# Attention on one core: product 2 of weights and V by seven smaller products, and VectorE's sums placed anew over a batch's four periods

## The chip, the core and the metric

The kernel runs on one core of a Trainium2 chip. PE is TensorE (matmuls), PEld its weight loads, DVE is VectorE, ACT is ScalarE, POOL is GpSimd, SP is SyncE, which here only issues DMAs. The metric is device time in microseconds (us), from the kernel's start to its end. One execution was profiled; the profile's "span" runs from its first to its last instruction.

## What is computed

Attention without a mask, for 8 batches of 2048 positions of width 512, in float32 at the borders:

```python
scores = q @ k.transpose(0, 2, 1) / sqrt(512)
weights = softmax(scores, axis=-1)
return weights @ v
```

## The kernel before

All products run on 16-bit copies of the inputs. Exponentials are taken without a maximum being subtracted, and rows are divided by their sum at the end; a column of ones beside V makes those sums.

**Two levels of seven products.** A product of two matrices, each cut into 2 x 2 blocks, is made by seven block products instead of eight, at the price of sums of blocks beforehand and of results afterwards (Strassen's method in Winograd's form). `Group` does it for scores, `Pair` for weights and V. A `Group` covers 2 x 128 keys and 1024 queries; each of its seven products is two matmuls of 512 columns (line 309). A `Pair` covers two query tiles of 128 and all of V; each of its seven products is eight matmuls of 256 columns (line 406; 257 where the column of ones goes along). The sums come before: `k_sums` (lines 185 to 188, in K's own tiles, one call for each of four quarters of K), `q_sums` (202 to 205), `v_sums` (219 to 222), `p_sums` of the exponentials (360 to 363). All of them run on DVE. A second level, `Fine` and `fine`, makes product 1 of the two pairs `a` and `b` of a period together: the two pairs' tiles and the two halves of V's block form a 2 x 2 scheme of their own, seven products of four matmuls with 128 columns (line 508), in four stages s1 to s4. Its sums are `a_sums` (486 to 489, into the tiles si) and `vi_sums` (233 to 236, into the tiles ti). Between the stages ACT copies parts of a PSUM bank (lines 516, 519, 523), and DVE adds two of them back (525, 528).

**Periods.** The main loop (line 776) runs over g = 0 to 31; four of them are a batch (`NQT` = 4). Period g makes the weights-and-V products of its two pairs, and beside them four `Group`s for the queries that come next. A period has 28 slots (`NS`). In each slot the loop issues, in this order: a product of the current or the previous group by `QORDER`; the exponential of the right half at the third position; the sums of `sums_of(g, slot)`; one product of a pair by `ORDER` (`pv`); and `prefetch`, which issues the next batch's loads and transposes by `PLAN` and, through a queue `background`, the sums of K:

```python
QORDER = ((0, 1), (1, 7), (0, 5), (0, 6), (1, 4), (0, 3), (0, 2))
ORDER = {
    1: "a7'", 3: "b7'", 5: "a4'", 7: "b4'", 8: "s1", 10: "a5", 11: "s2", 13: "b5", 14: "s3",
    16: "a3", 17: "s4", 18: "b3", 20: "a6", 22: "a2", 24: "b6", 26: "b2",
}
```

A pair (0, n) in `QORDER` is product n of the group begun in these seven slots, (1, n) one of the group before; "a7'" is product 7 of pair a of the period before. g = 0, 30 and 31 have orders of their own without `fine`. The schedule is manual: each engine executes its instructions in the order in which the program issues them. So an instruction that waits holds up everything behind it on its engine.

**What follows on the products.** Product 7 of a group is followed by a DVE add (331), product 3 by another (334); the two fill the tile cz, whose exponential (line 245, 1024 columns) ACT takes two positions later. Line 334 also empties the bank qz, of which there is one: product 5 of the next group starts in it. Line 331 reads the bank in which product 4 goes on. After products of a pair come reciprocals of the row sums (435, 441, 469), scaled copies on ACT (415) and the "final" on DVE (418: scale and add to the output tile o). When both halves of a tile are there, SP stores it (425).

**Loads.** POOL issues all loads of Q, K and V for the next batch (124, 211); Q and K go through two `stage` buffers, and SP issues the DMA that transposes a stage buffer into qraw or kraw (150). A stage buffer is free for the next load when its transpose has landed. `PLAN` puts these steps at (period of the batch, slot): K's quarters 0 to 3 are transposed at (1, 0), (1, 8), (1, 20) and (2, 7); K's third quarter is loaded at (1, 8), V's second at (1, 12). `KSUMS` adds four sums of K's quarters 0 to 3 to the queue at (1, 10), (1, 20), (2, 6) and (2, 20), and slots 2, 8, 10, 14, 16, 24 and 26 take one sum each from it.

**Start.** Batch 0 has its own beginning (lines 651 to 774): warm-up matmuls (697) on a zeroed tile, transposes on PE (137, 160), plain score tiles (252, 268), and a queue of sums that `step` takes from, among them the first of `v_sums`. In g = 0 the sums follow the table `SUMS0`.

Of the kernel before, what the change touches and what calls it, by code (L numbers as in the profile page):

```python
# [12 lines left out]
def kernel(  # L13
# [21 lines left out]
    nc = tc.nc  # L35
    P = 128
# [16 lines left out]
    CH = 4  # L53
    NCH = NKB // CH
    H = D // 2
    VP = D + 8
    TP = H + 8
    NG = NJ // 2
    NE = 6
    NI = NJ // 2  # L60
# [7 lines left out]
    opool = ctx.enter_context(tc.tile_pool(name="opool", bufs=6))  # L68
    small = ctx.enter_context(tc.tile_pool(name="small", bufs=2))
    czpool = ctx.enter_context(tc.tile_pool(name="czpool", bufs=2))  # L70
    psum = {}
    for name, bufs in (("qx", 2), ("qy", 1), ("qz", 1), ("px", 2), ("pz", 2)):
        psum[name] = ctx.enter_context(
# [7 lines left out]

    ctx.enter_context(tc.manual_schedule())

    ident32 = const.tile([P, P], F32)
    ident_dram = nc.inline_tensor(np.eye(P, dtype=np.float32), name="attn_identity")
    nc.scalar.dma_start(out=ident32[:], in_=ident_dram.ap())
    ident = const.tile([P, P], F16)

# [10 lines left out]
    vt2 = const.tile([P, NJ, H], F16, name="vt2")  # L101
    vt4 = const.tile([P, NJ, H], F16, name="vt4")
    si = {n: const.tile([P, NI, P], F16, name=f"si{n}") for n in (1, 2, 4)}
    ti = {n: const.tile([P, NI, P], F16, name=f"ti{n}") for n in (1, 2, 3, 4)}
    ci = const.tile([P, 2, P], F32, name="ci")
    staged = {}
    pts = {}

# [103 lines left out]

    def v_sums(b, c):
        vh = vraw[b % 2]
        js = slice(c * CH // 2, (c + 1) * CH // 2)
        b11, b12 = vh[:, js, 0, 0:H], vh[:, js, 0, H:D]
        b21, b22 = vh[:, js, 1, 0:H], vh[:, js, 1, H:D]
        return [
            lambda: sub(vt1[:, js, 0:H], b12, b11),
            lambda: sub(vt2[:, js], b22, vt1[:, js, 0:H]),  # L220
            lambda: sub(b12, b22, b12),  # L221
            lambda: sub(vt4[:, js], b21, vt2[:, js]),  # L222
        ]

    def vi_blocks(b):
        vh = vraw[b % 2]
        lo, hi = slice(0, NI), slice(NI, NJ)
        return vh[:, lo, 0, 0:P], vh[:, lo, 0, P:H], vh[:, hi, 0, 0:P], vh[:, hi, 0, P:H]

    def vi_sums(b):  # L230
        b11, b12, b21, b22 = vi_blocks(b)
        return [
            lambda: sub(ti[1][:], b12, b11),
            lambda: sub(ti[2][:], b22, ti[1][:]),
            lambda: sub(ti[3][:], b22, b12),
            lambda: sub(ti[4][:], b21, ti[2][:]),
        ]

    def new_p(sp):
# [234 lines left out]
            self.final(self.o1[:, H:D], self.x[:, 0:H], self.r1)  # L474
            self.store_first()

    def a_blocks(g):
        left = pts[g // 2][0][0]
        ca, cb = columns(g, "a"), columns(g, "b")
        lo, hi = slice(0, NI), slice(NI, NJ)  # L480
        return left[:, lo, ca], left[:, hi, ca], left[:, lo, cb], left[:, hi, cb]

    def a_sums(g):
        a11, a12, a21, a22 = a_blocks(g)
        return [
            lambda: add(si[1][:], a21, a22),
            lambda: sub(si[2][:], si[1][:], a11),
            lambda: sub(a21, a11, a21),
            lambda: sub(si[4][:], a12, si[2][:]),
        ]  # L490

    def fine(g, stage):

        a11, a12, a21, a22 = a_blocks(g)
        b11, b12, b21, b22 = vi_blocks(g // NQT)
        if stage == 1:
            for w in "ab":
                pairs[g, w] = Fine(g, w)
                pairs[g, w].x = bank("px")
        xa, xb = pairs[g, "a"].x, pairs[g, "b"].x  # L500

        def product(n, dst):
            lhs, rhs = {
                1: (a11, b11), 2: (a12, b21), 3: (si[4], b22), 4: (a22, ti[4]),
                5: (si[1], ti[1]), 6: (si[2], ti[2]), 7: (a21, ti[3]),
            }[n]
            for j in range(NI):
                nc.tensor.matmul(  # L508
                    dst, lhs[:, j, :], rhs[:, j, :],
                    start=(n == 1 and j == 0), stop=(j == NI - 1), skip_group_check=True,  # L510
                )

        if stage == 1:
            product(1, xb[:, 0:P])
            product(5, xb[:, P:H])
            nc.scalar.copy(out=xa[:, 0:H], in_=xb[:, 0:H])
        elif stage == 2:
            product(6, xb[:, 0:P])
            nc.scalar.copy(out=ci[:, 0, :], in_=xb[:, 0:P])
            product(2, xa[:, 0:P])  # L520
        elif stage == 3:
            product(7, xb[:, 0:P])
            nc.scalar.copy(out=ci[:, 1, :], in_=xb[:, 0:P])
            product(3, xa[:, P:H])
            nc.vector.tensor_add(xa[:, P:H], xa[:, P:H], ci[:, 0, :])
        else:
            product(4, xb[:, 0:P])
            nc.vector.tensor_add(xb[:, P:H], xb[:, P:H], ci[:, 1, :])

    pairs = {}  # L530

    def pv(g, which):
        if which[0] == "s":
            return fine(g, int(which[1]))
        g -= which.endswith("'")
        if which[1] == "1" and which[-1] != ">":
            pairs[g, which[0]] = Pair(g, which[0])
        part = {"<": (0, NJ // 2), ">": (NJ // 2, NJ)}.get(which[-1], ())
        pairs[g, which[0]].product(int(which[1]), *part)
# [2 lines left out]

    ORDER = {
        1: "a7'", 3: "b7'", 5: "a4'", 7: "b4'", 8: "s1", 10: "a5", 11: "s2", 13: "b5", 14: "s3",
        16: "a3", 17: "s4", 18: "b3", 20: "a6", 22: "a2", 24: "b6", 26: "b2",
    }
    FIRST = "a1< b1< a1> a5 b1> a3 a2 a6 - b5 - b3 b2 b6".split()
    ALONE = "a7' b7' a4' b4' a1 a5 b1 a3 b5 a6 b3 a2 a7 b6 a4 b2".split()
# [25 lines left out]
    ):  # L574
        PLAN.setdefault((qt_, slot_), []).append(what_)

    KSUMS = {(1, 10): 0, (1, 20): 1, (2, 6): 2, (2, 20): 3}
    background = deque()

    def prefetch(g, slot):  # L580
        b, qt = divmod(g, NQT)
        if (g, slot) == (0, 12):
            nc.gpsimd.memset(vraw[1][:, :, 1, D:D + 1], 1.0)
        for kind, what, c in PLAN.get((qt, slot), ()):
            if b + 1 < B:
                if kind == "load":
                    load_v(b + 1, c) if what == "v" else load(what, b + 1, c)
                else:
                    dma_transpose(what, b + 1, c)
        if (qt, slot) in KSUMS and b + 1 < B:  # L590
            background.extend(k_sums(KSUMS[qt, slot]))
        if background and slot in ((2, 8, 10, 14, 16, 24, 26)):
            background.popleft()()

    def sums_of(g, slot):

        if g == 0:
            return [first_sum(x) for x in SUMS0.get(slot, "").split()]
        todo = []
        inner = g < NP - 2  # L600
        bs = (8, 9, 10, 13) if inner else (7, 9, 11, 13)
        if inner and slot in (6, 7, 11, 12):
            todo.append(a_sums(g)[(6, 7, 11, 12).index(slot)])
        if slot in bs:
            todo.append(p_sums(g, "b")[bs.index(slot)])
        early = (20, 23, 25, 27) if g == NP - 2 else (19, 23, 25, 27)
        if slot in early and g + 1 < NP:
            todo.append(p_sums(g + 1, "a", 0, NJ if g % 2 == 0 else NE)[early.index(slot)])
        if slot in (4, 5) and g % 2 == 0:
            late = p_sums(g, "a", NE)  # L610
            todo.extend(late[0:2] if slot == 4 else late[2:4])
        sp = g // 2 + 2
        if slot in (23, 25, 27) and g % 2 == 1 and sp < NP // 2:
            todo.append(q_sums(sp)[(slot - 23) // 2])
        if slot == 6 and g % 2 == 0 and g < NP - 2:
            todo.append(q_sums(sp - 1)[3])
        if g % NQT == 0 and slot in VSUMS:
            n, c = divmod(VSUMS.index(slot), NCH)
            todo.append(v_sums(g // NQT, c)[n + 1])
        if g % NQT == NQT - 1 and g + 1 < NP:  # L620
            if slot in (14, 15, 16, 17):
                todo.append(v_sums(g // NQT + 1, slot - 14)[0])
            if slot in (18, 20, 21, 22):
                todo.append(vi_sums(g // NQT + 1)[(18, 20, 21, 22).index(slot)])
        return todo

    SUMS0 = {
        2: "v02", 3: "v03", 4: "q3", 5: "a0", 6: "a1", 8: "a3", 9: "a2",   # L630
        11: "v12 v13", 12: "v20 v21", 13: "v22", 14: "b0 v23", 15: "v30", 16: "b1 v31", 17: "v32",
        18: "v33", 19: "b3", 20: "k02", 21: "b2", 22: "A0", 23: "k12 A1", 24: "A2", 25: "k22 A3",
        26: "k32", 27: "t0 t1 t2 t3",
    }

    def first_sum(x):
# [3 lines left out]
        if x[0] == "q":  # L640
            return q_sums(1)[n]
        if x[0] == "t":
            return vi_sums(0)[n]
        return {
            "a": lambda: p_sums(0, "a", NG), "b": lambda: p_sums(0, "b"), "A": lambda: p_sums(1, "a")
        }[x[0]]()[n]

    TILES = (0, 2, 4, 5, 7, 9, 11, 13)
    VSUMS = (0, 1, 2, 3, 14, 15, 16, 17, 18, 20, 21, 22)

    warm = ti[4][:].rearrange("p j d -> p (j d)")
    nc.vector.memset(warm, 0.0)
    nc.gpsimd.memset(vt1[:, :, H:H + 1], 1.0)
    nc.gpsimd.memset(vraw[0][:, :, 1, D:D + 1], 1.0)

# [93 lines left out]
    for slot in range(14):  # L749
# [3 lines left out]
            background.extend(p_sums(0, "a", 0, NG))  # L753
            background.append(v_sums(0, 0)[0])
        if slot == 7:
            background.extend((v_sums(0, 1)[0], v_sums(0, 0)[1], v_sums(0, 1)[1]))
        if at == 0:
            cur = Group(0, 6 + n)
        if old == 0:
# [70 lines left out]
```

## Time and profile before

| | us |
|---|---|
| median of three runs | 799.06 |
| lowest and highest | 798.89, 799.32 |
| the profiled execution | 800.54 |
| its span | 798.7 |
| period g = 2 to 28, each | 24.16 |
| busy: PE, PEld | 791.7, 538.6 |
| busy: DVE, ACT, POOL | 622.2, 587.2, 72.2 |

In the profile an instruction's line is its place in the kernel's file; a row of the timeline gives start, duration, engine, line, operation, tiles (written <- read), shape and how many were merged, and in brackets the idle time of the engine before it and what ended it. The TensorE clock was granted in full (1.000). Matmuls are pipelined: a row's duration is longer than the time from its start to the next start, and it is the latter that counts. Period g starts at 63.34 us for g = 1 and at 88.43 for g = 2, and so on every 24.16.

### The profile page before, as it was taken

How to read it: one execution, taken by the hardware profiler on the slowest of the kernel's cores; microseconds unless marked ns; L12 is line 12 of the kernel's file. 1: busy time of each engine (PE TensorE's matmuls, PEld its weight loads, DVE VectorE, ACT ScalarE, POOL GpSimd, SP SyncE). 2: the span in 40 equal slices, each digit the busy share in tenths (PEclk: the TensorE clock that was granted, in tenths of full speed). 3: DMA queues.
4: the chain of work that ended last, by engine and by line, in shares of the span. 5: the costliest groups of instructions: out<-in, count | busy, mean ns of one | idle time of the engine just before them, and what ended most of it. 6: DMA issues, size and time to landing. Idle time of an engine off the chain costs nothing.

```text
span 798.7 us, 15575 instructions
## 1 busy us (share of the span) xinstructions
PE 791.7 (99%) x5878; PEld 538.6 (67%) x5878; DVE 622.2 (78%) x1426; ACT 587.2 (74%) x1107; POOL 72.2 (9%) x106
## 2 busy tenths in 40 slices
PE   9999999999999999999999999999999999999998
PEld 6556666666666666666666666666666666666676
DVE  2787869869698687977879787797878878788673
ACT  4677777877777787777777777777778777778842
POOL 4011010101100110001100111001110101000000
PEclk9999999999999999999999999999999999999999
DMA  9989993989929999389975799578994789910112
GB/s 221 177 144 160 196 181 86 168 141 193 189 57 179 163 195 172 74 165 155 202 146 105 150 178 193 116 126 148 188 205 87 144 150 195 160 53 32 49 60 101
DMA packets 188155, 115.90 MB, mean 145 GB/s; under 512 B 122288, under 2 KB 170800, under 8 KB 188080
## 3 DMA queue, kind: packets, MB, share of 16 engines
q0 software_dynamic: 49648, 49.29, 42.5%
q1 hardware_dynamic: 138144, 65.29, 36.8%
q8 instruction: 46, 0.75, 0.4%
q10 hardware_dynamic: 288, 0.33, 0.1%
q14 instruction: 29, 0.24, 0.1%
HBM read 100.73 MB, written 33.55 MB: 168 GB/s over the span
## 4 chain that ended last, share of the span: by engine, by line
PE 97%; DVE 1%; ACT 1%; issue 0%; DVEq 0%; ACTq 0%
PE t L309 45%; PE t L406 42%; PE t L508 6%; PE t L252 2%; PE tr L160 1%; PE tr L137 1%; PE t L697 0%; PE t L268 0%; DVE o L418 0%; DVE cz L334 0%; ACT left L245 0%; DVE vt L222 0%; DVE vh L221 0%; DVE s L360 0%; ACT o L415 0%
## 5 line engine op out<-in xcount | busy, mean ns | idle before, releaser
L309 PE MATMUL t<-qraw,kraw 128*128 128x512 f16 x728 | 197.0, 379 | 0.1
L406 PEld LDWEIGHTS <-s 128*128 128x128 f16 x1536 | 150.2, 98 | 57.6 <-issue 0.5
L245 ACT ACTIVATE left<-t 128x512 f16<-128x512 f32 (+1 forms) x260 | 156.1, 603 | 34.2 <-PE t L309 28.7
L415 ACT ACTIVATE o<-t,r 128x256 f32<-128x256 f32 x256 | 115.7, 481 | 62.6 <-DVE r L435 28.5
L406 PE MATMUL t<-vt,s 128*128 128x257 f16 (+1 forms) x1024 | 133.0, 273 | 0.0
L245 ACT ACTIVATE right<-cz 128x1024 f16<-128x1024 f32 x122 | 129.3, 1060 | 2.1 <-DVE cz L331 1.8
L309 PE MATMUL t<-qs,ks 128*128 128x512 f16 x488 | 130.6, 379 | 0.0
L309 PEld LDWEIGHTS <-kraw 128*128 128x128 f16 x976 | 93.0, 98 | 50.7 <-issue 0.7
L406 PEld LDWEIGHTS <-right 128*128 128x128 f16 x1024 | 100.2, 98 | 37.2 <-issue 0.5
L418 DVE SCALAR_TENSOR_TENSOR o<-t,r,o 128x256 f32<-128x256 f32 x192 | 92.2, 481 | 39.8 <-PE t L406 23.5
L325 ACT COPY cz<-t 128x512 f32<-128x512 f32 x120 | 70.2, 585 | 64.3 <-PE t L309 61.2
L331 DVE TENSOR_TENSOR cz<-t,cz 128x512 f32<-128x512 f32 x122 | 83.9, 688 | 36.7 <-PE t L309 36.3
L334 DVE TENSOR_TENSOR cz<-t,cz 128x512 f32<-128x512 f32 x122 | 84.0, 689 | 22.6 <-PE t L309 21.7
L309 PEld LDWEIGHTS <-ks 128*128 128x128 f16 x732 | 69.1, 98 | 46.7 <-issue 0.2
L320 ACT COPY t<-t 128x512 f32<-128x512 f32 x120 | 69.0, 575 | 20.0 <-PE t L309 17.7
L406 PE MATMUL t<-vh,left 128*128 128x256 f16 x560 | 72.9, 273 | 0.0
L309 PE MATMUL t<-qraw,ks 128*128 128x512 f16 x244 | 72.6, 379 | 0.0
L309 PE MATMUL t<-qs,kraw 128*128 128x512 f16 x244 | 72.6, 379 | 0.0
L328 ACT COPY cz<-t 128x512 f32<-128x512 f32 x122 | 70.8, 580 | 0.0
L406 PEld LDWEIGHTS <-left 128*128 128x128 f16 x560 | 54.8, 98 | 20.0
L406 PE MATMUL t<-vh,s 128*128 128x257 f16 x512 | 66.7, 273 | 0.4 <-ACT o L415 0.4
L406 PE MATMUL t<-vt,right 128*128 128x256 f16 x512 | 66.2, 273 | 0.3 <-DVE o L418 0.3
(85 smaller groups left out, 821.6 us busy)
## 6 DMA issues: line engine op xcount, KB each, us to landing
out_dram<-o SPq DMA_DIRECT2D x127, 256.0 KB, 3.0
vh<-in_v_dram POOLq DMA_DIRECT2D x32, 512.0 KB, 9.9
stage<-in_q_dram POOLq DMA_DIRECT2D x28, 512.0 KB, 6.9
stage<-in_k_dram POOLq DMA_DIRECT2D x28, 512.0 KB, 6.8
right<-in_q_dram POOLq DMA_DIRECT2D x2, 512.0 KB, 10.0
right<-in_k_dram POOLq DMA_DIRECT2D x2, 512.0 KB, 12.3
first<-in_q_dram SPq DMA_DIRECT2D x2, 256.0 KB, 3.5
cz<-in_q_dram SPq DMA_DIRECT2D x2, 256.0 KB, 4.8
```

Source lines behind the costliest of these rows:

```text
L245: nc.scalar.activation(out=out_, in_=in_, func=EXP, scale=inv_sqrt_d)
L252: nc.tensor.matmul(st[:], kops[c][0][:, n, dc, :], qraw[0][:, half * NT:(half + 1) * NT, dc, :], start=(dc == 0), stop=(dc == ND - 1),)
L309: nc.tensor.matmul(dst[:], lhs[:, j, dc, :], rhs[:, :, dc, :], start=(n in (1, 5) and dc == 0), stop=(dc == 1), skip_group_check=True,)
L320: f(out=self.y[:], in_=self.x[:])
L325: f(out=self.cz[:, 1, :], in_=self.z[:])
L328: nc.scalar.copy(out=self.cz[:, 0, :], in_=self.x[:])
L331: nc.vector.tensor_add(self.cz[:, 1, :], self.x[:], self.cz[:, 1, :])
L334: nc.vector.tensor_add(self.cz[:, 0, :], self.z[:], self.cz[:, 0, :])
L406: nc.tensor.matmul(dst[:, 0:width], lhs(j), rhs(j), start=(first and j == 0), stop=(j == NJ - 1), skip_group_check=True,)
L415: nc.scalar.activation(out=out_, in_=src, func=COPY, scale=r[:])
L418: nc.vector.scalar_tensor_tensor(out=out_, in0=src, scalar=r[:], in1=out_, op0=MULT, op1=ADD)
L508: nc.tensor.matmul(dst, lhs[:, j, :], rhs[:, j, :], start=(n == 1 and j == 0), stop=(j == NI - 1), skip_group_check=True,)
```

## The change

Product 2 of both pairs is made like product 1: `fine` gets an index s of the V half (0 for product 1, 1 for product 2), and the stages t1 to t4 (s = 1) take the place of a2 and b2. They stand at slots 21, 23, 25 and 27, and their results lie in the banks that a2 and b2 used. The final of line 418 that followed a2 and b2 follows stages t3 and t4. `a_sums` runs a second time a period, on the other half of the exponentials (in place there, too), into the same tiles si. `vi_sums` also runs for the second half; the tiles ti double in size, except that the third is now written into V's own tile, over a block that nothing reads any more (for the last batch, into the other buffer of V). The small float32 tile ci goes; its part is played by the left half of pair a's output tile. To make room in memory, the rows of V's tile get 514 elements instead of 520 (1028 bytes instead of 1040), those of vt1 258 instead of 264, and the two identity tiles and the warm-up tile share their memory with ti.

The sums of DVE are placed anew. `v_sums` works on halves (512 x 2 elements) instead of quarters, so there are half as many instructions, each twice as long. The sums of K leave the queue `background` and get fixed slots: quarter 0 at slots 11, 14, 15, 16 of period 1; quarter 1 at slots 18 and 20 of period 1 and 0 and 3 of period 2; quarter 2 at 11, 15, 18, 20 of period 2; quarter 3 at 0, 2, 4, 6 of period 3. `q_sums` move by one to three slots, the early `p_sums` of odd periods to slots 18, 21, 22 and 23. At the start, the second first-sum of V (half 1) is in the queue where the sum of quarter 1 was. The diff, cut to its core:

```diff
-    VP = D + 8
-    TP = H + 8
+    VP = D + 2
+    TP = H + 2
...
-    ti = {n: const.tile([P, NI, P], F16, name=f"ti{n}") for n in (1, 2, 3, 4)}
-    ci = const.tile([P, 2, P], F32, name="ci")
+    ti = {}
...
     def v_sums(b, c):
-        js = slice(c * CH // 2, (c + 1) * CH // 2)
+        js = slice(c * NI, (c + 1) * NI)
...
+    def t3_inner(b):
+        return vi_blocks(b + 1 if b + 1 == B else b)[1]
+
+    def vi_sums(b, s):
         b11, b12, b21, b22 = vi_blocks(b)
...
+                ti[n] = ipool.tile([P, 2, NI, P], F16, tag=f"t{n}", name=f"ti{n}")[:]
+        ti[3] = t3_inner(b)
+        at = lambda x: x[:, s]
         return [
+            lambda: sub(at(ti[1]), at(b12), at(b11)),
+            lambda: sub(at(ti[2]), at(b22), at(ti[1])),
+            lambda: sub(at(ti[3]), at(b22), at(b12)),
+            lambda: sub(at(ti[4]), at(b21), at(ti[2])),
         ]
...
-    def a_blocks(g):
-        left = pts[g // 2][0][0]
+    def a_blocks(g, s):
+        left = pts[g // 2][0][s]
...
-    def fine(g, stage):
+    def fine(g, s, stage):
...
+        pa, pb = (pairs.setdefault((g, w), Fine(g, w)) for w in "ab")
         if stage == 1:
+            for p in (pa, pb):
+                if s == 0:
+                    p.x = bank("px")
+                else:
+                    p.y = bank("pz")
+        xa, xb = (pa.y, pb.y) if s else (pa.x, pb.x)
...
-            nc.scalar.copy(out=ci[:, 0, :], in_=xb[:, 0:P])
+            nc.scalar.copy(out=pa.o2[:, 0:P], in_=xb[:, 0:P])
...
-            nc.vector.tensor_add(xa[:, P:H], xa[:, P:H], ci[:, 0, :])
+            nc.vector.tensor_add(xa[:, P:H], xa[:, P:H], pa.o2[:, 0:P])
+            if s:
+                pa.after2()
...
+            if s:
+                pb.after2()
...
-        16: "a3", 17: "s4", 18: "b3", 20: "a6", 22: "a2", 24: "b6", 26: "b2",
+        16: "a3", 17: "s4", 18: "b3", 20: "a6", 21: "t1", 23: "t2", 24: "b6", 25: "t3", 27: "t4",
...
-    KSUMS = {(1, 10): 0, (1, 20): 1, (2, 6): 2, (2, 20): 3}
+    KSUMS = {
+        divmod(slot, NS): (c, n)
+        for c, slots in (
+            (0, (39, 42, 43, 44)), (1, (46, 48, 56, 59)), (2, (67, 71, 74, 76)), (3, (84, 86, 88, 90))
+        )
+        for n, slot in enumerate(slots)
+    }
...
         if (qt, slot) in KSUMS and b + 1 < B:
-            background.extend(k_sums(KSUMS[qt, slot]))
-        if background and slot in ((2, 8, 10, 14, 16, 24, 26)):
-            background.popleft()()
+            c, n = KSUMS[qt, slot]
+            k_sums(c)[n]()
...
+        if g % 2 == 0 and sp < NP // 2:
+            put((2,), q_sums(sp)[2:])
+        if g % 2 == 1 and sp + 1 < NP // 2:
+            put((24, 26), q_sums(sp + 1))
+        if g % 2 == 0:
+            put((4, 4, 5, 5), p_sums(g, "a", NE))
+        if inner:
+            put((6, 7, 11, 12), a_sums(g, 0))
+            put((14, 17, 21, 22), a_sums(g, 1))
+        if g % 2 == 0 and sp < NP // 2:
+            put((7,), q_sums(sp)[3:])
+        put((8, 9, 10, 13) if inner else (7, 9, 11, 13), p_sums(g, "b"))
+        if g + 1 < NP:
+            if g % 2 == 0:
+                put((20 if g == NP - 2 else 19, 23, 25, 27), p_sums(g + 1, "a"))
+            else:
+                put((18, 21, 22, 23), p_sums(g + 1, "a", 0, NE))
+        if qt == 0:
+            put((0, 3), (v_sums(b, 0)[1], v_sums(b, 1)[1]))
+            put((15, 16), (v_sums(b, 0)[2], v_sums(b, 1)[2]))
+            put((18,), v_sums(b, 0)[3:])
+            if inner:
+                put((7, 11, 21, 17), vi_sums(b, 1))
+        if g == 1:
+            put((0, 2, 4, 6), vi_sums(0, 1))
+        elif qt == 1:
+            put((0,), v_sums(b, 1)[3:])
+        if qt == NQT - 1 and g + 1 < NP:
+            put((16, 18), (v_sums(b + 1, 0)[0], v_sums(b + 1, 1)[0]))
+            put((11, 14, 21, 23), vi_sums(b + 1, 0))
...
         if slot == 7:
-            background.extend((v_sums(0, 1)[0], v_sums(0, 0)[1], v_sums(0, 1)[1]))
+            background.extend((v_sums(0, 1)[0], v_sums(0, 0)[1]))
```

## The prediction

> **What bounds the kernel now.** I read the page first, then busy time by period, the PE timeline of one period, what PE waits for, and last the queues of DVE and DMA around the sums that move. A period is one value of g (28 slots); four make a batch, called periods 0 to 3 here, and "+17.0" means 17.0 us after a period's first matmul.
>
> ```profile
> PE 791.7 (99%) x5878; PEld 538.6 (67%) x5878; DVE 622.2 (78%) x1426; ACT 587.2 (74%) x1107; POOL 72.2 (9%) x106
> ```
>
> PE is the bound, and by its spacing it is at its floor. In the PE timeline a product of eight 256-column matmuls (line 406, 421.84 to 422.72) takes 0.87 us, so 109 ns each, and four of 128 columns (line 508, 409.84 to 410.07) take 0.224 us, so 56 ns each:
>
> ```profile
> 409.84 0.39 PE L508 MATMUL t<-vh,left 128*128 128x128 f16 x4
> 410.07 0.39 PE L508 MATMUL t<-ti,si 128*128 128x128 f16 x4
> 410.29 1.03 PE L309 MATMUL t<-qs,ks 128*128 128x512 f16 x4
> ...
> 421.84 1.04 PE L406 MATMUL t<-vh,left 128*128 128x256 f16 x8
> 422.72 1.03 PE L309 MATMUL t<-qs,ks 128*128 128x512 f16 x4
> ```
>
> From period g=2 to g=28 every period is 24.16 us long, to 0.01, with no PE wait that the profile names. The waits it names lie at the start, for instance:
>
> ```profile
> PE t L508 <- DVE si L489: 0.5, 1, 0.5
> PE t L406 <- ACT o L415: 0.4, 1, 0.4
> ```
>
> So removed PE time is gained in full, and new time appears only where a result comes after its slot. DVE is the engine to look at: busy time by period, for periods 0 and 1 of one batch (columns: us, PE, PEld, DVE, ACT, POOL busy, clock, DMA share, GB/s):
>
> ```profile
> 136.74:160.90 24.16, 24.16 (x182) 16.44 (x180) 21.35 (x52) 18.44 (x35) 2.22 (x3) 1.00 0.83 154
> 160.90:185.06 24.16, 24.16 (x182) 16.43 (x181) 16.97 (x38) 18.44 (x35) 2.22 (x3) 1.00 0.97 154
> ```
>
> **Second product by seven.** In 29 periods (g=1 to 29) two products 2 go, 16 matmuls x 109.2 ns = 1.747 us, and 28 matmuls x 55.9 ns = 1.564 us come. Gain 0.183 x 29 = **5.3 us**. That holds if the weight loads (98 ns a row, line 508) stay hidden, as under the first product's 28. The Trainium skill ("TensorE: Matmul & The Clock Gate", Back-to-back issue gap) speaks against it: streams of a weight load and a 128-column matmul are said to sustain about 81 ns a matmul. By that, an estimate, the t stages would cost 2.27 us, a loss of 15. The trace disagrees: 56 ns between the same kind of operands, so I keep 5.3.
>
> **What DVE and ACT get.** Per period DVE gets four 512-element f16 sums (0.335 us apart, e.g. 411.25 to 411.59) and two adds of 0.21: 1.76 us; period 0 also four sums for V's lower half (1.34) and one q sum (0.60), and twelve V sums of 0.335 become five of 0.60 (-1.0). So period 0 goes from 21.35 to about 24.0 of 23.97 us by busy rows, which count some 0.09 us after each instruction in which the next could already run (0.69 long, 0.60 from start to start); by starts (0.60, 0.39, 0.335, 0.21, 0.08) it is 22.1. It fits, barely. Walking the queue by these starts, the last add and final of stage t4 end 1.6 to 1.8 us into the next period. The first result needed there, line 331 of slot 1, ends at about +3.1; PE needs it at +3.47 (product 4, slot 4). ACT gets 0.36+0.28+0.27 us a period; each copy of a t stage ends 0.25 to 0.4 us before the matmul that overwrites its source. I charge none of this, with 0 to 5 us as bound (7 crossings into period 0, 29 t stages; nothing below zero, since nothing is freed). The row pitch of V falls from 1040 to 1028 bytes, which no row shows; nearest is the 257-column row at the 256-column price. I take 0, at most 1 us on a V load.
>
> **K's sums move past a DMA.** This decides. Sums that a background queue fed at fixed slots get fixed places. For K's second quarter of the next batch the first sum (line 185) goes from slot 26 of period 1 to slot 18. What it reads is written by the transpose that SP issues at slot 8. Of batch 1, SP's timeline, and the DMA issues of a window around 169.2 (last number: us from issue to landing):
>
> ```profile
> 161.62 1.83 SPq L150 DMA_TRANSPOSE kraw<-stage  x1
> 166.81 2.07 SPq L425 DMA_DIRECT2D out_dram<-o  x2
> 169.01 13.10 SPq L150 DMA_TRANSPOSE kraw<-stage  x2
> ```
>
> ```profile
> kraw<-stage SPq DMA_TRANSPOSE x1, 13.4
> ```
>
> It lands at 182.4, **+21.5**. The DVE timeline shows when slot 18 comes (the reciprocal of line 469 closes it) and when the old order read it:
>
> ```profile
> 177.88 0.17 DVE L469 RECIPROCAL r<-t 128x1 f32<-128x1 f32 x1 [0.94 <-PE t L406]
> 178.38 0.69 DVE L334 TENSOR_TENSOR cz<-t,cz 128x512 f32<-128x512 f32 x1 [0.33 <-PE t L309]
> ...
> 185.94 0.42 DVE L185 TENSOR_TENSOR ks<-kraw 128x512 f16<-128x512 f16 x1
> ```
>
> Now it was read at +25.0; after the change DVE reaches it at +17.1 and stands still. The same windows give issue plus landing for batches 0 to 6, as offsets in period 1: 14.9, 21.5, 20.4, 21.4, 19.7, 20.1, 20.9. Batch 0 is early (5.2 us of transfer); the six others wait 2.6 to 4.4 us. Behind the sum stands line 334 of slot 19, which empties the bank qz that product 5 of slot 23 starts in. Product 5 was at 181.15 (+20.25); without a2 (0.87) and with t1 (0.45) it is at +19.83. With the transpose landing at L the bank is free at L + 0.02 + 0.35 + 0.69 + 0.06 = L + 1.12 (75.33 to 75.35 in batch 0; a sum and its neighbour's start; line 334; DVE's end to PE's start at 77.05 to 77.11). So PE loses L - 18.71. Then DVE still has a6's final, the second K sum, one si sum and one early sum (0.39 + 0.335 + 0.335 + 0.46) ahead of line 331, which ends at L + 3.2; ACT's exp of cz (1.06) waits for it, and t2's copy stands behind that until L + 4.5, while t3's product 7, which overwrites the copy's source, is due at L + 3.7: another 0.8. At the landings of before: (2.8 + 1.7 + 2.7 + 1.0 + 1.4 + 2.2) + 6 x 0.8 = 11.7 + 4.8 = **16.5 us**.
>
> L itself moves. The transpose of K's first quarter (161.62) is behind the store of o1 on SP; that store follows the last final, 1.3 us later than now. The loads of K's third and V's second quarter wait for its landing and take the DMA engines while our transpose runs. They end up to 1.3 us later; L moves by 0 to 1.3. I take 0.7, since part of the shift lets our transfer go first: 6 x 0.7 = 4.2. Sum **20.7 us**, bounds 16.5 to 24.3.
>
> **Start.** V's first sums now take halves. The second, at 38.08, needs all four V loads; the last is issued at 15.27 and lands 24.8 us later, at 40.0:
>
> ```profile
> vh<-in_v_dram POOLq DMA_DIRECT2D x1, 512.0 KB, 24.8
> ```
>
> DVE stands from 38.3 to 40.1 in front of the copy at 38.56, whose bank a plain tile of 40.52 needs: 0.9 us of PE, then line 331 at 45.0 instead of 43.05 and ACT's exp behind it: I count **1.2** (0.5 to 2). Later in g=0 V's sums are 0.3 us shorter, taken off the 0.9 us of PE gaps at 56 to 60; in g=1 K's first sum moves behind the si sum that PE waited for at 76: another -0.35 of 0.9.
>
> **Sum:** -5.3 + 20.7 + 1.2 - 0.3 - 0.35 = **+15.9 us**. The profiled execution took 800.54 us (span 798.7 and 1.8 around it), 1.5 over the median of the three runs; I add the difference to the median: 799.06 + 15.9 = **815.0**.
>
> **Rivals.**
> 1. *The transpose lands in time* (13%): the other side. In batch 0 the two loads didn't fall on it and it landed at +14.9. If the loads start after it, because their release comes some 2.5 us later, the stall is nil below L = 18.7 and its echo soon after: 799.06 - 5.3 + 0.55 = 794.3. For it: the release does move later; against: by 1.3 us, and SP's place for our transpose, +8.1, stays.
> 2. *It lands part of the way earlier* (10%): each us is 6 us; 797 to 807.
> 3. *DVE and ACT are too full as well* (11%): 7 crossings into period 0 with 0.3 us of margin and 29 t stages: up to 5 more with the landings at their late end, 820 to 828.
> 4. *Weight loads show in the t stages* (1%): 28 x 98 ns against 1.747 us is +1.0 a period, +29 instead of -5.3: 849. Line 508's 56 ns excludes it unless operands differ.
> 5. *The clock drops in the long stall* (4%): at the very start the 512-column matmuls of line 697 come 0.43 us apart against 0.216 later, so a cold spell of some 3.4 us costs 1.7; twice (batches 1 and 3, 3.5 us alone): 818. The Trainium skill (same page, What's actually happening) has the clock halve after an idle window of about 3.4 us; no stall in this trace is that long.
>
> **Numbers.** Forecast (61%): 807 to 820. Range 801 to 824: it leaves out rival 1, the upper part of 3, rival 4 and some of 2. Faster by over 0.2% (the bound of what a measurement here tells from no change): rival 1 and a little of 2, 0.14; within: 0.03; slower: 0.83.
>
> **What would show it.** In the profile after: line 185 on DVE with idle before it, released by DMA kraw<-stage, six times 2.5 to 5 us; PE waiting on DVE line 334 (or ACT) six times, once a batch in period 1; other periods 23.97 us long; line 219 waiting for vh's DMA at 38. If the long periods are not period 1, or line 185 doesn't wait, the forecast is wrong; if all periods are over 23.97, rival 3 holds.

## The result and the profile after

The changed kernel takes 825.33 us (median of four runs, 824.14 to 829.15) beside 798.97 for the kernel before: a ratio of 1.0337, 95% interval 1.0302 to 1.0372. It is slower by 26.4 us. The direction was forecast, with 815.0; the time lies just outside the range given, 801 to 824. The profiled execution took 824.57 us, with a span of 822.5 against 798.7, so the trace has 23.8 us to explain.

The page of the changed kernel shows PE no longer full, and a DMA in the chain that ended last:

```profile
PE 792.6 (96%) x6226; PEld 537.8 (65%) x6226; DVE 677.8 (82%) x1568; ACT 609.1 (74%) x1194; POOL 72.1 (9%) x106
PE 79%; DMA 16%; DVE 3%; ACT 1%; issue 1%; POOL 0%; DVEq 0%; ACTq 0%
```

Lines from the changed kernel carry its own numbers: 317 was 309 (score products), 342 and 339 were 334 and 331 (the adds into cz), 414 was 406, 519 was 508, 477 was 469 (reciprocal), 497 was 489 (a sum of `a_sums`), 530 was 519 (copy in stage 2), 253 was 245 (exponential); 185 is still K's first sum.

Period 3 of batch 0 and periods 0 and 1 of batch 1 of the changed kernel (g = 3 to 5; the columns are us, then PE, PEld, DVE, ACT and POOL busy, the clock, the DMA share and GB/s):

```profile
116.49:140.50 24.01, 24.01 (x195) 16.41 (x193) 21.22 (x51) 19.24 (x39) 0.74 (x1) 1.00 0.54 108
140.50:164.61 24.11, 24.11 (x195) 16.41 (x193) 23.07 (x54) 19.18 (x39) 2.22 (x3) 1.00 0.81 154
164.61:191.68 27.07, 24.34 (x196) 16.40 (x193) 20.08 (x48) 19.24 (x39) 3.70 (x5) 1.00 0.93 158
```

Only period 1 is long, once a batch: 28.11, 27.07, 28.55, 30.03, 27.15, 26.90 and 27.78 us in batches 0 to 6; all others of g = 1 to 29 are 24.01 or, in period 0, 24.11. What PE waited for, in the order engine, tile and line, total us, times, longest:

```profile
PE t L317 <- DVE cz L342: 19.2, 7, 4.2
PE t L519 <- ACT o L530: 3.0, 5, 0.6
```

Seven waits for the add that frees bank qz, and five for the copy of stage t2. The transpose of K's second quarter in batch 1 (DMA issues at its start), the DVE timeline around slot 18, and PE:

```profile
kraw<-stage SPq DMA_TRANSPOSE x1, 12.9
```

```profile
181.62 0.17 DVE L477 RECIPROCAL r<-t 128x1 f32<-128x1 f32 x1 [0.48 <-PE t L414]
185.70 0.42 DVE L185 TENSOR_TENSOR ks<-kraw 128x512 f16<-128x512 f16 x1 [3.90 <-DMA kraw<-stage]
186.04 0.68 DVE L342 TENSOR_TENSOR cz<-t,cz 128x512 f32<-128x512 f32 x1
...
188.17 0.68 DVE L339 TENSOR_TENSOR cz<-t,cz 128x512 f32<-128x512 f32 x1
```

```profile
184.04 0.59 PE L317 MATMUL t<-qraw,kraw 128*128 128x512 f16 x2
186.78 0.59 PE L317 MATMUL t<-qs,ks 128*128 128x512 f16 x2 [2.14 <-DVE cz L342]
...
188.96 0.59 PE L317 MATMUL t<-qs,kraw 128*128 128x512 f16 x2
190.15 0.39 PE L519 MATMUL t<-vh,left 128*128 128x128 f16 x4 [0.59 <-ACT o L530]
```

The transpose lands at 185.7, +21.1 in the period. DVE stands for 3.9 us with the sum at its head; line 342 runs only then, and PE's next product starts 2.31 us late (186.78 - 184.04, less the 0.43 of two matmuls). The second gap, 0.75 us by the same count, is product 7 of t3 behind the copy on ACT, which itself stands behind the exponential that waits for line 339:

```profile
188.88 1.06 ACT L253 ACTIVATE right<-cz 128x1024 f16<-128x1024 f32 x1 [0.89 <-DVE cz L339]
189.85 0.25 ACT L530 COPY o<-t 128x128 f32<-128x128 f32 x1
```

### The profile page after: what moved, and what is told of

Its sections match the earlier page's. It is cut to its first block, busy times and chain, and to the rows that moved or that the text cites. A ratio compares the mean times of both kernels' runs of the same rounds, so it can differ in the third digit from the quotient of the medians.

```text
span 822.5 us, 16565 instructions
## 1 busy us (share of the span) xinstructions
PE 792.6 (96%) x6226; PEld 537.8 (65%) x6226; DVE 677.8 (82%) x1568; ACT 609.1 (74%) x1194; POOL 72.1 (9%) x106
## 4 chain that ended last, share of the span: by engine, by line
PE 79%; DMA 16%; DVE 3%; ACT 1%; issue 1%; POOL 0%; DVEq 0%; ACTq 0%
PE t L317 38%; PE t L414 31%; DMA kraw<-stage 12%; PE t L519 10%; DMA vh<-in_v_dram 3%; DMA right<-in_q_dram 1%; ACT right L253 1%; DVE cz L342 1%; DMA first<-in_k_dram 1%; DVE cz L339 0%; DVE o L426 0%; DVE s L369 0%; DVE left L496 0%; DVE kraw L186 0%; POOL stage L124 0%
## 5 line engine op out<-in xcount | busy, mean ns | idle before, releaser
L317 PE MATMUL t<-qraw,kraw 128*128 128x512 f16 x728 | 206.4, 379 | 0.2 <-ACT left L253 0.2
L317 PE MATMUL t<-qs,ks 128*128 128x512 f16 x488 | 136.1, 381 | 19.2 <-DVE cz L342 19.2
L414 PE MATMUL t<-vt,s 128*128 128x257 f16 (+1 forms) x1024 | 135.6, 275 | 0.0
L317 PEld LDWEIGHTS <-kraw 128*128 128x128 f16 x976 | 90.5, 98 | 44.9 <-issue 1.0
L317 PEld LDWEIGHTS <-ks 128*128 128x128 f16 x732 | 66.6, 97 | 59.7 <-issue 21.3
L339 DVE TENSOR_TENSOR cz<-t,cz 128x512 f32<-128x512 f32 x122 | 83.7, 686 | 22.2 <-PE t L317 21.5
L519 PEld LDWEIGHTS <-left 128*128 128x128 f16 x928 | 69.2, 98 | 45.4 <-issue 5.2
L342 DVE TENSOR_TENSOR cz<-t,cz 128x512 f32<-128x512 f32 x122 | 83.8, 687 | 13.7 <-PE t L317 7.1
L328 ACT COPY t<-t 128x512 f32<-128x512 f32 x120 | 69.0, 575 | 20.0 <-PE t L317 15.9
L519 PE MATMUL t<-vh,left 128*128 128x128 f16 x696 | 67.6, 219 | 3.0 <-ACT o L530 3.0
## 6 DMA issues: line engine op xcount, KB each, us to landing
right<-in_k_dram POOLq DMA_DIRECT2D x2, 512.0 KB, 12.1
```

Of the source, the lines that this page charges most:

```text
L317: nc.tensor.matmul(dst[:], lhs[:, j, dc, :], rhs[:, :, dc, :], start=(n in (1, 5) and dc == 0), stop=(dc == 1), skip_group_check=True,)
L328: f(out=self.y[:], in_=self.x[:])
L339: nc.vector.tensor_add(self.cz[:, 1, :], self.x[:], self.cz[:, 1, :])
L342: nc.vector.tensor_add(self.cz[:, 0, :], self.z[:], self.cz[:, 0, :])
L414: nc.tensor.matmul(dst[:, 0:width], lhs(j), rhs(j), start=(first and j == 0), stop=(j == NJ - 1), skip_group_check=True,)
L519: nc.tensor.matmul(dst, lhs[:, j, :], rhs[:, j, :], start=(n == 1 and j == 0), stop=(j == NI - 1), skip_group_check=True,)
```

## Experiments

The theory: VectorE's queue stands at slot 18 of period 1 for a DMA that has not landed, and everything else about the change is a gain or near to nothing. Rival 1: VectorE is simply too full with the second product's sums. Rival 2: the small products are dear in themselves. All edits are to the changed kernel unless another is named. Ratios are to the kernel before, run on the same chip. A diff shows of a line only the part that matters.

**1. The sums of K's second quarter late again** (`k_sums_late`).

```diff
-(1, (46, 48, 56, 59))
+(1, (54, 58, 64, 66))
```

> The changed kernel with the four sums of K's quarter 1 back at slot 26 of period 1 and slots 2, 8 and 10 of period 2; all else as changed. If the loss is VectorE standing still at slot 18 for the transpose (theory), the seven long first periods (27 to 30 us) fall to about 24.0, PE waits on line 342 vanish, and of the 23.8 us of extra span some 27 go: 795 to 797 us, faster than before by 0.3 to 0.5%. If VectorE is too full with the second product (rival 1), the stalls only move to another slot or period: over 805. If the seven products themselves are dear (rival 2), over 800 with no stall to see.

Measured: 797.55 us, ratio 0.9976 (0.9966 to 0.9985). Four places of sums take 27.8 us away. Its periods 0 and 1 of batch 1, with the second product and all its sums in them:

```profile
136.46:160.58 24.12, 24.12 (x195) 16.42 (x193) 23.08 (x54) 19.19 (x39) 2.22 (x3) 1.00 0.81 154
160.58:184.59 24.01, 24.01 (x195) 16.40 (x193) 19.85 (x47) 19.25 (x39) 2.22 (x3) 1.00 0.91 158
```

DVE does the same work as in the changed kernel, is busy for 23.08 of 24.12 us in period 0, and PE loses 0.1 us there. Rival 1 is out. The transpose still lands at +21.0 to +22.1 in this run; it is merely read later.

**2. The early sums alone, in the kernel before** (`before_k_sums_early`). The sums of quarter 1 leave the queue for the slots that the change gives them:

```diff
-KSUMS = {(1, 10): 0, (1, 20): 1, (2, 6): 2, (2, 20): 3}
+KSUMS = {(1, 10): 0, (2, 6): 2, (2, 20): 3}
+PINNED = {(1, 18): 0, (1, 20): 1, (2, 0): 2, (2, 3): 3}
...
+        if (qt, slot) in PINNED and b + 1 < B:
+            k_sums(1)[PINNED[qt, slot]]()
```

> The kernel before with one edit: the sums of K's quarter 1 at slots 18 and 20 of period 1 and 0 and 3 of period 2 instead of the queue. Theory: with the landings of before (+19.7 to +21.5) product 5 of slot 23, here at +20.25, loses L + 1.12 - 20.25 in six batches: 2.4 + 1.3 + 2.2 + 0.6 + 1.0 + 1.7 = 9 us, none in batch 0 if that still lands at +14.9; no echo, since there is no stage t3: 806 to 811 us. Rival 1 (VectorE too full): no change, 799, as nothing was added to VectorE.

Measured: 812.42 us, ratio 1.0160 (1.0146 to 1.0174), above what was expected. The loss appears without any work added. What PE waited for (same columns as above, lines of the kernel before):

```profile
PE t L309 <- DVE cz L334: 7.3, 6, 2.6
PE t L309 <- DVE cz L331: 2.7, 6, 0.5
```

The first row is the stall of the formula: PE loses 2.7, 2.2, 0.5, 1.2, 0.2, 0.6 and 1.0 us in batches 0 to 6. The last six make 5.7 us, less than the 9 expected, because the transpose landed earlier in all of them (+19.4 to +21.3). Three things were not foreseen. Batch 0 was not spared: there the transpose landed at +21.9, although nothing ahead of it differs from the profiled kernel before, in which it landed at +14.9. In period 2 of six batches 0.62 us each goes to the second row, because the two sums at slots 0 and 3 delay line 331. And in batch 1 the granted clock is at half for 3.4 us after the stall, which costs another 1.7 us.

**3. One load out of the transpose's way** (`v_load_after_k`).

```diff
-(1, 12, "load", "v", 1)
+(1, 17, "load", "v", 1)
```

> The changed kernel, sums of K as changed, but the load of V's quarter 1 for the next batch issued after that of K's quarter 3, which itself waits for the transpose in question. If the transpose is late because two loads share the DMA engines with it, it has one load beside it instead of two (0.5 instead of 1.05 MB): landing at +15 to +18 instead of +21 to +23, nothing or under 1 us a batch lost: 795 to 802 us. If its lateness has another cause (its own issue, the stores ahead of it), landings and time stay: 822 to 826.

Measured: 802.56 us, ratio 1.0039 (1.0026 to 1.0053). The landings move from +20.9 to +23.1 to +18.4 to +19.4 in batches 1 to 6 (+17.3 in batch 0): 2.8 us earlier on the mean, less than expected. The load that shares the engines does count, but with one beside it the transpose still takes 10.9 us in batch 1:

```profile
stage<-in_k_dram POOLq DMA_DIRECT2D x1, 512.0 KB, 10.1
kraw<-stage SPq DMA_TRANSPOSE x1, 10.9
```

**4. The transpose two slots earlier** (`transpose_earlier`).

```diff
-(1, 8, "trans", "k", 1)
+(1, 6, "trans", "k", 1)
```

> The changed kernel with its sums as changed (first sum of K's quarter 1 at slot 18), but the transpose of that quarter issued two slots earlier, at slot 6 of period 1, some 2 us before, so that it is on its way before the loads of K's third and V's second quarter, which start about +7.4. If it is late because it stands behind and between their packets (theory), it lands at +10 to +15, ahead of slot 18 (+17.1), PE loses nothing and the time is 796 to 799 us. If it lands at about +19 (2 us earlier, the same 13 us of transfer), the time is 801 to 806. If the stores ahead of it on SP or its own issue set the pace: over 815.

Measured: 797.05 us, ratio 0.9973 (0.9964 to 0.9983). Issued 1.7 us earlier (+6.35 instead of +8.09), ahead of POOL's loads at +7.4 and +8.1, the transpose lands some 8 us earlier, at +13.1 to +15.8 in batches 1 to 6 (+16.6 in batch 0). Its issue on SP and the time to landing in batch 1:

```profile
166.96 2.25 SPq L150 DMA_TRANSPOSE kraw<-stage  x1
```

```profile
kraw<-stage SPq DMA_TRANSPOSE x1, 7.2
```

It takes 7.2 us where it took 12.9. With that, K's early sums cost nothing at slot 18: the lateness of this transpose is what VectorE paid for. What in its new place makes it fast is not separated. The edit also puts the transpose ahead of the second store that SP issues (at +8.7 here, at +7.65 in the changed kernel). And to be issued before the loads is not enough by itself: in batch 0 of the changed kernel the transpose is issued at +8.4 and the first load 1.0 us later, as here, and it takes 13.7 us.

**5. Product 2 by eight again** (`no_product_2`): as experiment 1, and

```diff
-21: "t1", 23: "t2", 24: "b6", 25: "t3", 27: "t4",
+22: "a2", 24: "b6", 26: "b2",
...
-            put((14, 17, 21, 22), a_sums(g, 1))
...
-            if inner:
-                put((7, 11, 21, 17), vi_sums(b, 1))
...
-        if g == 1:
-            put((0, 2, 4, 6), vi_sums(0, 1))
-        elif qt == 1:
+        if qt == 1 and g > 1:
```

> As k_sums_late (K's sums late), but product 2 by eight matmuls of 256 columns again, a2 and b2 at slots 22 and 26, without the second run of the sums on exponentials and V blocks. The second product alone is then the difference to k_sums_late: by matmul spacing 0.183 us in each of 29 periods, 5.3 us: this one 800 to 802, periods 24.16 to 24.19 instead of 24.01. Rival 2: no difference, or this one is the faster.

Measured: 802.34 us, ratio 1.0032 (1.0019 to 1.0044), 4.8 us above experiment 1. Its periods are 24.19 us, 0.18 longer than 24.01, which is the gain forecast from spacing; 7 x 0.1 us of period 0 come off. Rival 2 is out. Period 2 of batch 1:

```profile
185.35:209.54 24.19, 24.19 (x181) 16.38 (x180) 19.98 (x47) 18.32 (x35) 3.65 (x5) 1.00 1.13 187
```

**6. The start** (`late_and_start`): as experiment 1, and

```diff
-            background.extend((v_sums(0, 1)[0], v_sums(0, 0)[1]))
+            background.append(v_sums(0, 0)[1])
...
-        2: "v11", 4: "q3", ...
+        2: "v01", 3: "v11", 4: "q3", ...
```

> k_sums_late, and at the start the first sum of V's second half not in the queue before the main loop but at slot 2 of period 0 (its second sum at slot 3), where all of V has landed. Theory: VectorE no longer stands for V's last load (2.0 us at 38 in the changed kernel's profile), the PE gap of 1.2 us at 40 goes and period 1 starts some 1 us earlier, at 63.3 instead of 64.3: 796.5 us, 0.1% under k_sums_late. Rival: the sums now crowd period 0 and the gaps at 57 to 60 grow by as much: 797.5.

Measured: 796.52 us, ratio 0.9960 (0.9947 to 0.9972). Its interval and that of experiment 1 overlap, so the time alone doesn't settle it; the trace does for the place. In the changed kernel DVE waits for V's last load, and a plain tile on PE for the copy behind it:

```profile
39.96 0.69 DVE L219 TENSOR_TENSOR vt<-vh 128x1024 f16<-128x1024 f16 x1 [1.95 <-DMA vh<-in_v_dram]
```

```profile
41.31 1.02 PE L260 MATMUL t<-qraw,kraw 128*128 128x512 f16 x4 [1.04 <-DVE qraw L163]
```

Both waits are absent here, and period 1 starts at 63.10 us instead of 64.31 in experiment 1. It is then 0.55 us longer than there (24.68 for 24.13), which takes half of that back. The reason is not the start: in this execution the transpose of K's first quarter landed at +12.1 instead of +8.6, DVE stood for it, and PE waited for the sum of line 497 behind it:

```profile
75.22 0.42 DVE L185 TENSOR_TENSOR ks<-kraw 128x512 f16<-128x512 f16 x1 [1.35 <-DMA kraw<-stage]
```

In experiment 7, with the same start, it landed at +8.4; period 1 starts at 62.43 and is 24.10 us long.

**7. The rows of vt1 at 264 elements again** (`late_start_pitch`): as experiment 6, and

```diff
-    TP = H + 2
+    TP = H + 8
```

> late_and_start, and the rows of the tile vt1 back at 264 elements (528 bytes, a multiple of 16) instead of 258 (516 bytes). In the changed kernel's trace the 257-column matmuls that read vt1 come 112 ns apart instead of 110, 16 of them a period; those that read V's own tile with rows of 1028 bytes stay at 110. If the row pitch of vt1 is the cause, periods fall from 24.01 to 23.98, 1.0 us in all: 795.5. If it is something else in the period, nothing changes.

Measured: 795.24 us, ratio 0.9948 (0.9935 to 0.9962): the fastest version here, 0.5% faster than the kernel before. Its interval, too, overlaps that of the experiment ahead of it; the periods show the gain, 23.98 us for 24.01. Period 3 of batch 0:

```profile
110.51:134.49 23.98, 23.98 (x195) 16.39 (x193) 21.21 (x51) 19.25 (x39) 0.74 (x1) 1.00 0.65 122
```

**8. The shorter rows alone, in the kernel before** (`before_pitch`).

```diff
-    VP = D + 8
-    TP = H + 8
+    VP = D + 2
+    TP = H + 2
```

> The kernel before with the shorter rows alone (V's tile 514 elements, vt1 258). If the pitch of vt1 is the cause of the 112 ns, periods are 24.19 instead of 24.16 and the 257-column matmuls on vt1 come 112 ns apart; the DMAs into V's tile land as before: 800.0 us. If not: 24.16 and 799.

Measured: 800.7 us in a single run, and periods of 24.19. The time of one run says little; the spacing does. The 257-column matmuls on vt1 come 112 ns apart with rows of 516 bytes (here and in experiment 6) and 110 with 528 (kernel before and experiment 7). Those on V's own tile come 110.7 ns apart on the mean with rows of 1028 bytes, after 110.0 with 1040.

## Why the prediction was right in its cause and short in its size

By the trace, span against span, the terms of the sum measured:

| term | forecast | measured |
|---|---|---|
| product 2 by seven | -5.3 | -5.3 (29 x 0.18, experiment 5) |
| vt1's rows | 0 | +0.9 (29 x 0.03) |
| DVE and ACT fuller | 0 | +0.7 (7 x 0.1) |
| K's sums, batches 1 to 6 | +20.7 | +23.4 |
| K's sums, batch 0 | 0 | +4.1 |
| start, to the first slot of g = 1 | +0.9 | +1.0 |
| old gaps of g = 1 | -0.35 | -0.9 |
| sum | +15.9 | +23.9, of 23.8 |

**Right:** the place, the queue behind it and the price of it. The stall was put at L - 18.71; in batch 1, L = 21.06 gives 2.35 and PE lost 2.31. The echo on ACT was put at 0.8 and is 0.75. The shift of the landings by the later store of o1 was put at 0.7 us; the six landings are 21.6 on the mean after 20.7, 0.9 later. The first transpose of period 1, which starts this chain, is issued 1.8 us later where 1.3 was put; in experiment 5, where it is issued as early as before, the six landings are 20.5 on the mean, against 21.5 in experiment 1. Experiments 1 and 4 remove the whole loss by changing the two sides of this one wait.

**Failed: "Batch 0 is early (5.2 us of transfer); the six others wait".** It waits as well: the landing is at +22.1, and the period 4.1 us too long. Period 1 of batch 0, and K's first sum in it:

```profile
64.36:92.48 28.12, 24.46 (x195) 16.38 (x192) 21.26 (x53) 19.06 (x39) 2.96 (x4) 1.00 1.14 151
86.49 0.43 DVE L185 TENSOR_TENSOR ks<-kraw 128x512 f16<-128x512 f16 x1 [4.83 <-DMA kraw<-stage]
```

The +14.9 belonged to that execution, not to the batch. K's first quarter happened to land at +12.0 there, so the two loads that wait for it came only 2.9 us after the transpose of the second quarter had been issued. The same happened in experiment 6: +12.1, and the second quarter at +15.0. In the eight other profiled executions K's first quarter lands between +8.1 and +9.3, the loads follow 0.6 to 1.4 us after the transpose, and the second quarter lands between +16.2 and +22.1. Among these are experiments 2 (+21.9) and 8 (+18.3), which up to there differ from the kernel before in nothing or in the row pitch alone. What decides between 16 and 22 is open. I took a landing that had one odd value out of seven for a property of the batch.

**Mis-sized: the six other batches,** 23.4 for 20.7. Of the 2.7, 1.5 is the landings: they moved by 5.7 us in all, against 6 x 0.7 = 4.2. With the measured landings, L - 18.71 + 0.8 gives batches 1, 4, 5 and 6 each 0.09 too much, and batches 2 and 3 too little by 0.82 and 0.83; that is the other 1.3. In these two it is rival 5, which I had as an alternative to the forecast when it comes on top of it. The stretches behind the long stalls of batches 2 and 3:

```profile
286.60:290.70 4.10, 4.10 (x22) 2.54 (x22) 4.10 (x10) 2.28 (x4) 1.61 (x3) 0.58 0.87 123
388.70:392.60 3.90, 3.90 (x22) 2.33 (x22) 3.90 (x10) 2.28 (x4) 1.67 (x3) 0.62 0.89 117
```

The granted clock is 0.58 and 0.62 in them: in each, a spell of 3.41 us at half speed begins 0.7 and 1.0 us after matmuls resume. Each costs 1.7 us as priced, of which 0.75 would have been the echo, so 0.9 net. The 256-column matmuls of b6 come 213 ns apart there instead of 109. Which stalls trip it is not a matter of length alone: stalls of 2.87 and 4.35 us did, 3.23 and 3.02 did not, and in experiment 2 one of 2.19 did and one of 2.71 did not. The Trainium skill ("TensorE: Matmul & The Clock Gate", What's actually happening) has the clock halve after an idle window of about 3.4 us, in windows that run freely. The length of the spell agrees (3.41 us), but here stalls shorter than such a window, 2.19 and 2.87 us, were followed by one. The four runs, 824.1 to 829.2 us, differ in mean clock too (0.996 to 0.986, the slowest run lowest), which speaks for more or fewer such spells; only the first of them has a trace, so that part is argued, not shown.

**Also:** the rule of the Trainium skill ("TensorE: Matmul & The Clock Gate", Back-to-back issue gap), some 81 ns for a weight load and a 128-column matmul, did not come true: the matmuls come 56 to 57 ns apart in the t stages of the changed kernel, too. VectorE was busy for 23.07 us in period 0, where 24.0 had been reckoned from rows. The row pitch, taken at 0 for want of a row, was worth 0.9 us, on the rows of vt1, which the forecast did not weigh, and not on the V loads that I bounded. The last two rows of the table ahead of its sum hold luck: the 0.9 us of old gaps was DVE waiting for the landing at +12.0 in the profiled kernel before, and in experiment 8, where it is at +8.7, there is no such gap (24.20 us). Where the landing was late again, in experiment 6, the new order left 0.55, the 0.9 less 0.35 of the forecast. Period 1 of batch 0 starts between 62.6 and 63.4 us in the three traces with the old start, and between 64.3 and 64.9 in the five with the changed one. The +26.4 of the medians is 2.6 more than the spans' 23.8: the profiled execution of before was itself 1.5 us over its median, and the changed kernel's profiled run 0.8 under its own.

## What to carry to other kernels

An instruction that needs a DMA's result is placed by the transfer's landing, and where an engine executes in program order, everything behind it pays; so move such a step only after its slack has been read off the latest of many landings, not off a typical one. When it must come early, look first at what shares the DMA engines: 1.7 us earlier at the issue, ahead of two loads and a store, was 8 us at the landing. And price a long stall of PE with the half-speed spell that may follow it on top, not as another case.

## What was not expected of the hardware

- A 257-column read from rows of 516 bytes costs 2 ns a matmul (112 for 110 with rows of 528), from rows of 1028 bytes 0.7 (110.7 for 110.0 with 1040); why the two differ is open.
- A half-speed spell of PE's clock of 3.41 us can follow a stall as short as 2.19 us, and can stay out after one of 3.23.
- The time to landing of one and the same transpose, issued at slot 8, varied between 5.2 and 15.0 us. One load less beside it made it 2.8 us shorter on the mean (experiment 3); the shares of the other transfers were not separated.
